# Weight sums through DRAM: the 16 GpSimd transfers written with the 128 rows outermost and the weight pairs inside

## The chip, the cores and the metric

One core of one Trainium2 chip runs the kernel. The metric is the device time of one execution in microseconds; it is the median of several runs. A profiled execution adds a page and a trace, whose times are counted in microseconds from the start of the span.

## What is computed

A decoder block over 1040 positions (16 meta tokens and 1024 tokens) of width 1024, all in float32:

```python
p = h @ w_in + b_in                     # columns: u_s5 | q | k | v | o | i | f | g_s5 | g_m
y_s5 = GLU(GELU(S5(u_s5)))              # grouped complex-diagonal state space model
y_m = (sigmoid(o) * HeadNorm(mLSTM(q, k, v, i, f))) @ m_w_out
mix = sigmoid(g_s5) * y_s5 + sigmoid(g_m) * y_m
h = LN(alpha * h + mix @ w_o)
h = LN(alpha * h + relu(h @ w_up + b_up)^2 @ w_down)
```

## The kernel before

Each float32 operand of the large products is split in two parts (`hi`, rounded, and `lo`, the rest), and a product is three matmuls, at L226, L227 and L228. TensorE (PE in the profile) runs these nearly without a gap. ScalarE (ACT) makes the `hi` parts, VectorE (DVE) the `lo` parts, so a weight tile `wraw` becomes `whi` (L212) and `wlo` (L213).

The two largest projections of the middle of the block, the mLSTM gate `g_m` and the output `m_w_out`, use seven products of half blocks in place of eight (class `Seven`). For that, sums and differences of weight blocks are needed. They are made without any compute engine: `w_sums` sends 16 DMA transfers from GpSimd's queue (POOL), from DRAM to DRAM into `ws_dr`, some of which copy and some of which add to what is there (`accum_op=OP.add`). There are eight for three pairs of tiles of `wf` (s = 0) and eight for four pairs of `wmo` (s = 1). One is issued with every second weight job from the fifth on: ahead of it POOL copies one element of the job's `whi` into `mark`, which makes POOL wait for that job. `Seven.load` fetches the results with SP's queue from about 698 us on.

All other bulk transfers are issued from SP's queue, one after the other in program order. Each takes one of eight completion semaphores in turn, and waits until the transfer that used it last has landed. So one slow transfer stops the queue eight transfers later.

Besides the jobs, the kernel runs side lanes, whose instructions a scheduler places between the matmuls. Three are spoken of here:
- The gates of the mLSTM (`gates`), near 100 to 150 us: short DVE and ACT steps on `gts`, with three small transposes on PE into `gps` (L421 is the last), then `gB` and `wiB` fetched by SP. Next to it `s5_pre` fetches the parameters `s_lam` of the state space model (L583), and DVE's first step with them is L557.
- `s5_gelu` for the fourth batch, near 566 to 598 us: `ys_dr` is stored, fetched back as `s5yc` in eight pieces (L871), put through GELU (`gelf`), and split into `gelh` (ACT) and `gell` (DVE, L878), on which the first job of the GLU waits.
- `ah_scale`, from about 528 us: eight row tiles `ahr` are fetched (L1377), multiplied and added (two DVE instructions at L1386), and stored to `ah_dr` (L1388). `up_early` follows it, on `wur`, `wpre` and `wu_dr`.

The GLU jobs (`z2s`, L940 to L945) use ACT and DVE to empty PE's accumulators; DVE's instructions stand in one fixed order, so an `ahr` that is late holds up a `z2s`.

Of the kernel before, what the change touches and what calls it, by code (L numbers as in the profile page):

```python
# [14 lines left out]
P = 128  # L15

D = 1024
KT = D // P
# [94 lines left out]
def decoder_block(  # L113
# [24 lines left out]
    def f32(ap):  # L138
        return ap.bitcast(F32)
# [816 lines left out]
    ws_dr = dram.tile([7, 4, P, 512], F32, name="ws_dr")  # L956

    def w_sums():
        todo = {}
        for s, (n0, p0, w, i0) in enumerate(((3, 0, wf, JGM + NM), (4, 3, wmo, 0))):  # L960
            def src(r, kh):
                return bass.AP(tensor=w.tensor, offset=w.offset + (i0 + r) * KT * P * P + 512 * kh,
                               ap=[[2 * KT * P * P, n0], [KT * P, P], [1, 512]])
            a11, a12, a21, a22 = src(0, 0), src(0, 1), src(1, 0), src(1, 1)
            d = [ws_dr[p0:p0 + n0, i] for i in range(4)]
            todo[s] = [(d[0], a21, 0), (d[2], a11, 0), (d[0], a22, 1), (d[2], a21, 1), (d[1], d[0], 0), (d[1], a11, 1),
                       (d[3], d[1], 0), (d[3], a12, 1)]
        mark = const.tile([1, 1], F32, name="mark")
        for s, i in ((0, 0), (0, 1), (0, 2), (0, 3), (0, 4), (1, 0), (0, 5), (1, 1), (0, 6), (1, 2), (0, 7), (1, 3),
                     (1, 4), (1, 5), (1, 6), (1, 7)):  # L970
            job = yield
            g_.tensor_copy(mark, f32(job.w[0][0][0:1, 0:1]))
            d, a, add = todo[s][i]
            tc.keep_in_program_order(g_.dma_start(d, a, accum_op=OP.add) if add else g_.dma_start(d, a))
# [442 lines left out]
    for w in ORDER.split():  # L1417
        n, i = w[0], int(w[1:])
# [22 lines left out]
    for w in LOAD0.split():  # L1441
        i = int(w[1])
# [21 lines left out]

    jobs = all_jobs
    ws = w_sums()
    next(ws)
    begin, first, run7 = gates_and_output()
# [609 lines left out]
```

## Time and profile before

| what | value |
|---|---|
| median of 3 runs | 1566.78 us (1564.85 to 1566.83) |
| the profiled execution, its own time | 1566.04 us |
| its span | 1564.2 us |
| PE busy | 1515.8 us, 97% |
| DVE busy, ACT busy, POOL busy | 1079.9, 642.7, 102.2 us |
| mean granted clock of PE | 0.984 |
| transfers of `w_sums` | 16, from 74.5 us to 602.1 us |

In the profile a line number is a line of the kernel. A row of the timeline gives the start, the duration, the engine, the line, the operation and its tiles; in brackets stands how long the engine sat idle before it and what ended that. SPq is SP's queue, and its rows are issues of transfers, not the moving of data. In a list of queues, q1 is what SP issued and q0 what POOL issued: packets, megabytes, and the share of the time of all 16 DMA engines.

### The profile page before, as it was taken

What the parts mean: (1) busy time and instruction counts of PE and PEld (TensorE: products, weight loads), DVE (VectorE), ACT (ScalarE), POOL (GpSimd) and SP (SyncE); (2) the same over time, 40 slices, a digit from 0 to 9 for tenths busy, and PEclk for the clock granted to TensorE, in tenths of its full rate; (3) what the DMA queues carried; (4) which work ended last, traced back from release to release, by engine and by line L of the source; (5) the groups of instructions that cost most, each with busy time, mean ns of one, the idle gap of its engine ahead of it and who ended that gap; (6) DMA issues with size and microseconds to landing.
All of it is one profiled execution on the core that took longest, in us unless ns stands there. A gap on an engine that the chain in (4) does not pass through costs nothing.

```text
span 1564.2 us, 20543 instructions
## 1 busy us (share of the span) xinstructions
PE 1515.8 (97%) x7593; PEld 1278.7 (82%) x7593; DVE 1079.9 (69%) x2083; ACT 642.7 (41%) x982; POOL 102.2 (7%) x195
## 2 busy tenths in 40 slices
PE   8999999998999998989999999999999999999997
PEld 8998988996878886768788887888888888888886
DVE  7667555659867845677789675666666679766786
ACT  6523353333355433325534324444444534433340
POOL 0000001124031200000000001000000000000000
PEclk9999999998999999989999999999999999999999
DMA  8412324414354556775353328644443798667642
GB/s 311 159 57 61 100 62 129 122 37 112 104 129 103 164 182 218 279 269 195 108 170 114 108 76 247 225 158 149 147 149 123 248 363 322 230 229 236 216 166 108
DMA packets 137509, 261.32 MB, mean 167 GB/s; under 512 B 30768, under 2 KB 52984, under 8 KB 137352
## 3 DMA queue, kind: packets, MB, share of 16 engines
q1 hardware_dynamic: 111344, 233.00, 43.7%
q0 software_dynamic: 26064, 27.01, 7.1%
q8 instruction: 60, 0.98, 0.3%
q14 instruction: 41, 0.34, 0.1%
HBM read 188.78 MB, written 84.55 MB: 175 GB/s over the span
## 4 chain that ended last, share of the span: by engine, by line
PE 31%; issue 23%; DMA 3%; DVE 2%; ACT 0%; SPq 0%; POOL 0%; POOLq 0%; DVEq 0%
PE mm L228 7%; PE mm L227 7%; PE mm L226 7%; PE sd L227 3%; PE sd L226 3%; PE sd L228 3%; DMA wpre<-wu_dr 1%; DMA rawb<-h_dr 1%; DMA wu_dr<-wpre 1%; DMA wur<-in_wup_dram 0%; DVE wlo L1043 0%; DVE wlo L213 0%; DMA woraw<-in_wo_dram 0%; POOL wpre L1621 0%; SPq L991 0%
## 5 line engine op out<-in xcount | busy, mean ns | idle before, releaser
L226 PE MATMUL mm<-hT_hi,whi 128*128 128x512 f32 (+3 forms) x604 | 231.0, 382 | 8.0 <-ACT whi L1042 5.4
L228 PE MATMUL mm<-hT_hi,wlo 128*128 128x512 f32 (+3 forms) x604 | 226.7, 380 | 5.7 <-DVE wlo L213 3.7
L227 PE MATMUL mm<-hT_lo,whi 128*128 128x512 f32 (+3 forms) x604 | 229.1, 379 | 0.0
L226 PEld LDWEIGHTS mm<-hT_hi,whi 128*128 128x128 f32 x604 | 115.7, 192 | 26.6 <-ACT whi L1042 6.2
L228 PEld LDWEIGHTS mm<-hT_hi,wlo 128*128 128x128 f32 x604 | 115.0, 191 | 25.5 <-DVE wlo L213 4.3
L227 PEld LDWEIGHTS mm<-hT_lo,whi 128*128 128x128 f32 x604 | 115.6, 191 | 17.6 <-issue 0.4
L227 PE MATMUL sd<-dwl,dah 128*128 128x512 f32 x240 | 94.5, 394 | 0.0
L228 PE MATMUL sd<-dwh,dal 128*128 128x512 f32 x240 | 94.4, 394 | 0.0
L226 PE MATMUL sd<-dwh,dah 128*128 128x512 f32 x240 | 94.2, 393 | 0.0
L1773 ACT ACTIVATE dah<-da 128x1024 fp32r<-128x1024 f32 x56 | 58.7, 1052 | 86.2 <-PE sd L227 38.9
L1777 ACT ACTIVATE dwh<-wdr 128x1024 fp32r<-128x1024 f32 x56 | 58.9, 1053 | 84.0 <-DMA wdr<-in_wdn_dram 27.5
L1774 DVE TENSOR_TENSOR dal<-da,dah 128x1024 fp32r<-128x1024 f32 x56 | 68.2, 1219 | 23.8 <-ACT dah L1773 23.3
L228 PE MATMUL mm<-dwh,dal 128*128 128x512 f32 (+1 forms) x224 | 84.5, 378 | 0.0
L226 PE MATMUL mm<-dwh,dah 128*128 128x512 f32 (+1 forms) x224 | 84.4, 377 | 0.0
L227 PE MATMUL mm<-dwl,dah 128*128 128x512 f32 (+1 forms) x224 | 84.3, 377 | 0.0
L1778 DVE TENSOR_TENSOR dwl<-wdr,dwh 128x1024 fp32r<-128x1024 f32 x56 | 68.2, 1219 | 13.1 <-ACT dwh L1777 12.4
L226 PE MATMUL mm<-whi,hT_hi 128*128 128x256 f32 (+1 forms) x256 | 75.2, 294 | 0.0
L228 PE MATMUL mm<-whi,hT_lo 128*128 128x256 f32 (+1 forms) x256 | 74.7, 292 | 0.0
L227 PE MATMUL mm<-wlo,hT_hi 128*128 128x256 f32 (+1 forms) x256 | 73.8, 288 | 0.0
L213 DVE TENSOR_TENSOR wlo<-wraw,whi 128x1024 fp32r<-128x1024 f32 (+1 forms) x46 | 56.1, 1222 | 19.1 <-ACT whi L212 18.6
L228 PE MATMUL mm<-th,wul 128*128 128x512 f32 x156 | 61.6, 395 | 0.0
L227 PE MATMUL mm<-tl,wuh 128*128 128x512 f32 x156 | 61.5, 394 | 0.0
(474 smaller groups left out, 3703.1 us busy)
## 6 DMA issues: line engine op xcount, KB each, us to landing
da<-act_dr SPq DMA_DIRECT2D x56, 512.0 KB, 5.4
wdr<-in_wdn_dram SPq DMA_DIRECT2D x56, 512.0 KB, 6.3
wur<-in_wup_dram SPq DMA_DIRECT2D x32, 512.0 KB, 4.3
act_dr<-upy SPq DMA_DIRECT2D x64, 256.0 KB, 2.5
wraw<-in_wf_dram SPq DMA_DIRECT2D x30, 512.0 KB, 6.9
wu_dr<-wpre SPq DMA_DIRECT2D x21, 512.0 KB, 4.7
wpre<-wu_dr POOLq DMA_DIRECT2D x21, 512.0 KB, 5.0
act_dr<-upx SPq DMA_DIRECT2D x32, 256.0 KB, 2.8
```

Of the source, the lines that this page charges most:

```text
L213: todo.append(lambda e=v_, r=r, hi=hi, lo=lo, n=n: e.tensor_tensor(lo[:, :n], r[:, :n], f32(hi[:, :n]), op=OP.subtract))
L226: t_.matmul(ps, ah, bh, start=(i == 0 and part[0]), stop=False, skip_group_check=skip)
L227: t_.matmul(ps, ah, bl, start=False, stop=False, skip_group_check=skip)
L228: t_.matmul(ps, al, bh, start=False, stop=(i == n - 1 and part[1]), skip_group_check=skip)
L1773: a_.activation(ah[:, :D], a[:, :D], AF.Copy)
L1774: v_.tensor_tensor(alo[:, :D], a[:, :D], f32(ah[:, :D]), op=OP.subtract)
L1777: a_.activation(wh, raw[i], AF.Copy)
L1778: v_.tensor_tensor(wl, raw[i], f32(wh), op=OP.subtract)
```

## The change

Only the access patterns of the 16 transfers change. Before, the outermost dimension of both sides is the pair (3 or 4 of them), then 128 rows, then 512 numbers. After, the 128 rows are outermost, the pairs come second, and the 512 numbers stay innermost. The same numbers go to the same places.

```diff
             def src(r, kh):
                 return bass.AP(tensor=w.tensor, offset=w.offset + (i0 + r) * KT * P * P + 512 * kh,
-                               ap=[[2 * KT * P * P, n0], [KT * P, P], [1, 512]])
+                               ap=[[KT * P, P], [2 * KT * P * P, n0], [1, 512]])
             a11, a12, a21, a22 = src(0, 0), src(0, 1), src(1, 0), src(1, 1)
-            d = [ws_dr[p0:p0 + n0, i] for i in range(4)]
+            d = [ws_dr[p0:p0 + n0, i].rearrange("n p c -> p n c") for i in range(4)]
```

The instructions of PE, DVE, ACT and SP stand in the same order as before, and so do POOL's. What differs is the shape of 16 of POOL's rows. The first piece is from POOL's order near 198 to 235 us of the profile; `v_...` are tiles of the mLSTM's values.

```order
 L972 COPY mark<-whi 1x1
-L974 DMA ws_dr<-in_wf_dram 3x128x512
+L974 DMA ws_dr<-in_wf_dram 128x3x512
 L336 MEMSET v_2267 128x1 x4
 L336 MEMSET v_3375 16x1
 L972 COPY mark<-whi 1x1
 L336 MEMSET v_2268 128x1 x4
-L974 DMA ws_dr<-ws_dr 3x4x16384
+L974 DMA ws_dr<-ws_dr 128x3x512
```

Nothing moved. A transfer within `ws_dr` used to have both inner dimensions in one run of 65536 numbers per pair, cut into four pieces of 16384; now it has 384 pieces of 512.

The second piece is the end of POOL's order, near 524 to 602 us.

```order
-L974 DMA ws_dr<-ws_dr 4x4x16384
+L974 DMA ws_dr<-ws_dr 128x4x512
 L972 COPY mark<-whi 1x1
-L974 DMA ws_dr<-in_wmo_dram 4x128x512
+L974 DMA ws_dr<-in_wmo_dram 128x4x512
 L972 COPY mark<-whi 1x1
-L974 DMA ws_dr<-ws_dr 4x4x16384
+L974 DMA ws_dr<-ws_dr 128x4x512
 L972 COPY mark<-whi 1x1
-L974 DMA ws_dr<-in_wmo_dram 4x128x512
+L974 DMA ws_dr<-in_wmo_dram 128x4x512
```

Nothing moved here either: two copies and two additions, each behind the `mark` of its job.

## The prediction

> **What bounds the kernel now.** I read the page first, then who waits for the 16 transfers, then PE's waits from 70 to 640 us, the time in which they run.
>
> ```profile
> PE 1515.8 (97%) x7593; PEld 1278.7 (82%) x7593; DVE 1079.9 (69%) x2083; ACT 642.7 (41%) x982; POOL 102.2 (7%) x195
> ```
>
> PE is the bound. The change touches no instruction of PE, DVE, ACT or SP, so it can gain only where PE stands still, or runs at a lower clock after standing still, because something came late through a DMA. What `ws_dr` holds is fetched from 698 us on, long after the last transfer, so nobody waits for the sums themselves. What counts is what the transfers do to others while they run.
>
> How long two of the copies and one of the additions take (issue time at the end of the first line, landing in the second):
>
> ```profile
> L974 POOL DMA_DIRECT2D ws_dr<-in_wf_dram x1: 1112/1112/1112, 104.2 to 104.2; - x1
> DMA to landing us min/median/max: 13.7/13.7/13.7
> ...
> L974 POOL DMA_DIRECT2D ws_dr<-in_wmo_dram x1: 1129/1129/1129, 267.7 to 267.7; - x1
> DMA to landing us min/median/max: 13.1/13.1/13.1
> ...
> L974 POOL DMA_DIRECT2D ws_dr<-in_wmo_dram x1: 1946/1946/1946, 490.3 to 490.3; - x1
> DMA to landing us min/median/max: 29.6/29.6/29.6
> ```
>
> Three pairs (768 KB) take as long as four (1024 KB): the time goes with the bytes of one pair, 256 KB, as if each pair had one DMA engine of its own. An addition takes twice as long. The queues say the same, here for 112.5 to 113, 113 to 113.5 and 115 to 115.5 us, beside a small fetch on SP's queue (q1):
>
> ```profile
> DMA packets 108, 0.06 MB, mean 115 GB/s; under 512 B 98, under 2 KB 98, under 8 KB 108
> q0 software_dynamic: 10, 0.04, 19.9%
> q1 hardware_dynamic: 98, 0.02, 18.7%
> ...
> DMA packets 9, 0.04 MB, mean 74 GB/s; under 512 B 0, under 2 KB 0, under 8 KB 9
> q0 software_dynamic: 9, 0.04, 18.0%
> ...
> q1 hardware_dynamic: 6, 0.00, 1.1%
> ```
>
> POOL's queue is busy 18 to 20% of 16 engines: 3 of 16 is 18.75%. And the fetch of SP sends 98 packets in the first half microsecond, then none, and its last few two microseconds later. I read that as follows: its share on the 13 free engines is done at 113, its share on the 3 others waits behind POOL's packets.
>
> [...]
>
> **What one engine's queue costs others, first place (A).** The small fetch is `s_lam`. SP, DVE, PE, and PE's clock there (the columns of the window: PE, PEld, DVE, ACT, POOL, clock, DMA share, GB/s):
>
> ```profile
> 111.48 0.33 SPq L583 DMA_DIRECT2D s_lam<-in_s5l_dram  x1
> ...
> 117.13 0.17 DVE L557 TENSOR_SCALAR s_t<-s_lam 128x16 f32<-128x16 f32 x1 [3.62 <-DMA s_lam<-in_s5l_dram]
> ...
> 124.75 0.27 PE L421 MATMUL gps<-ident,gts 36*128 36x36 f32 x1 [1.99 <-ACT gts L418]
> ...
> 120.00:130.00 10.00, 8.01 (x49) 6.99 (x48) 4.51 (x25) 5.72 (x9) 0.00 (x0) 0.83 0.20 58
> ...
> 147.75 0.70 PE L477 MATMUL pu<-v,kw 16*128 16x257 f32 x2 [1.47 <-ACT kw L460]
> ```
>
> DVE stands 3.62 us for `s_lam`. Its next steps, and ACT's after them, run without a gap up to the `gts` for which PE stands 1.99 us; then the clock is 0.83 over 10 us, 1.7 us lost. Together 3.7 us. The `kw` at 147.75 hangs on the same chain, through `gB`, fetched after `gts`.
>
> **Second place (B).** The fourth `s5_gelu` and `ah_scale`. A copy is issued at 570.1, now in 64 KB pieces, as the packets of an earlier one at 400 to 403 us show (0.33 MB in 5):
>
> ```profile
> q0 software_dynamic: 5, 0.33, 25.2%
> ...
> L974 POOL DMA_DIRECT2D ws_dr<-ws_dr x1: 588/588/588, 570.1 to 570.1; - x1
> DMA to landing us min/median/max: 13.5/13.5/13.5
> ```
>
> It lands at 583.6. What SP, DVE and PE do meanwhile (the landing is that of the store at 571.26):
>
> ```profile
> 571.26 0.32 SPq L1388 DMA_DIRECT2D ah_dr<-ahr  x1
> DMA to landing us min/median/max: 13.3/13.3/13.3
> ...
> SPq L871 <- DMA ah_dr<-ahr: 7.5, 1, 7.5
> ...
> 585.27 0.34 SPq L1377 DMA_DIRECT2D ahr<-ah_dr  x1
> 586.65 1.36 SPq L198 DMA_DIRECT2D wraw<-in_wglu_dram  x1
> 588.06 0.59 SPq L1377 DMA_DIRECT2D ahr<-ah_dr  x1
> ...
> 589.98 1.23 DVE L1386 TENSOR_TENSOR ahr<-ahr,gB 128x1024 f32<-128x1024 f32 x1 [14.80 <-DMA ahr<-ah_dr]
> 597.42 1.22 DVE L878 TENSOR_TENSOR gell<-gelf,gelh 128x1024 fp32r<-128x1024 f32 x1
> 602.86 1.23 DVE L1386 TENSOR_TENSOR ahr<-ahr,gB 128x1024 f32<-128x1024 f32 x1 [4.22 <-DMA ahr<-ah_dr]
> 605.37 0.69 DVE L944 TENSOR_TENSOR z2s<-mm,z2s 128x512 f32<-128x512 f32 x1
> ...
> 598.69 0.50 PE L227 MATMUL mm<-gell,whi 128*128 128x512 f32 x1 [3.15 <-DVE gell L878]
> 606.12 0.79 PE L226 MATMUL mm<-gelh,whi 128*128 128x512 f32 x1 [2.13 <-DVE z2s L944]
> ...
> 600.00:605.00 5.00, 3.99 (x12) 2.77 (x10) 2.11 (x2) 1.53 (x3) 2.08 (x2) 0.73 0.65 204
> 605.00:610.00 5.00, 3.88 (x10) 3.12 (x11) 4.06 (x6) 0.00 (x0) 0.00 (x0) 0.66 0.80 172
> ```
>
> The store lands at 584.5, a microsecond after the copy. SP's last piece of `s5yc` waits 7.5 us for it, and the `ahr` fetch behind it goes out at 585.27. DVE stands 14.80 us, does three pairs of `ahr` steps, then `gell`, for which PE stands 3.15 us; the last `ahr` holds up `z2s`, for which PE stands 2.13 us. With the lower clock (5 us at 0.73 and at 0.66, 3.0 us) 8.3 us are lost here.
>
> **The change, part by part.**
>
> POOL's issue. A transfer from `wf` or `wmo` has as many pieces of 512 as before: nothing. The four copies within `ws_dr` go from 12 or 16 pieces to 384 or 512; their issue may grow from 0.588 us to the 1.129 or 1.946 us of the others, at most 1.4 us each. POOL is 7% busy, and its next work waits for a later job: nothing, and if that cover were gone, 6 us of POOL's time.
>
> Landing of one transfer. No row has a DRAM-to-DRAM transfer on 16 engines. The nearest have 128 rows outermost, one on POOL's own queue with 512 KB, one on SP's with 1024 KB:
>
> ```profile
> wpre<-wu_dr POOLq DMA_DIRECT2D x21, 512.0 KB, 5.0
> wdr<-in_wdn_dram SPq DMA_DIRECT2D x8, 1024.0 KB, 9.7
> ```
>
> So a copy lands in 5 to 9.7 us in place of 13 to 14, an addition, at twice that, in 10 to 19 in place of 30. I take 6 and 11, nearer to the first, since that row is of the same queue.
>
> A. The copy issued at 104.2 is gone at 110, before `s_lam` goes out at 111.48. `s_lam` then lands at about 113.4, when its free engines had finished, and DVE's 3.62 us are gone. With 9.7 us the copy ends at 114 and DVE still gains about 2. PE cannot gain more than its 3.7 us, nor more than `kw` comes earlier, since it stands for that next: 3.6, between 2 and 3.6. The stretches behind it, up to 560 us, have DVE steps that themselves follow PE, so the gain is carried on.
>
> B. Without the 7.5 us wait the `ahr` fetch goes out at 577.8, lands after 589.98 - 585.27 = 4.7 us, and the first two pairs are over early. But the third `ahr`, at 588.06, stands behind a fetch of weights (586.65) that waits for PE's progress. It lands at 588.06 + 4.7 = 592.8, its pair takes (597.42 - 589.98) / 3 = 2.5 us, `gell` starts at 595.2, not 597.42: 2.2 us earlier. The last `ahr` is fetched after that pair is stored, so it and `z2s` come 2.2 us earlier too. PE gets to `z2s` sooner and stands there longer: what counts is the 2.2 at 606.12, not 3.15 + 2.13. Bounds: 0, if the third `ahr` lands no earlier, and the whole 8.3.
>
> Behind 610 us up to 698 PE waits little for anything but `begin`'s fetches, issued after the last transfer: nothing, though stores there may come out of the way earlier (0 to 2 in the range).
>
> Sum: 3.6 + 2.2 = 5.8 us from the profiled execution's own 1566.04, so 1560.2. The median lies 0.74 higher, so 1561.0.
>
> **The rivals.**
>
> Given back. The gain of A is used up where DVE itself is the limit, and B's next late step takes the place of the one removed. For it: PE's stall at `z2s` does grow. Against it: DVE ahead of those stretches waits for PE. The gain is then 0 to 2.2: 1565.6.
>
> All of B. If the `ahr` fetches come early enough that neither stall remains, 3.6 + 8.3 = 11.9: 1554.9. Against it: the third fetch's place behind the weights.
>
> Slower: all 16 engines together are slower than the three were. Now 768 KB in 13.7 us are 56 GB/s; below that the point is passed. At 48 GB/s, 16 us, `s_lam` comes 2.3 us later and the store in B too, on all engines: 2.3 + 2.3, so 1571.4. Against it: four pairs move a third more than three in the same time, so the sum has not been the limit. [...]
>
> No effect: the transfers stay on few engines: 1566.8. Against it: the two rows just quoted.
>
> **How the numbers follow.** The forecast 0.61, given back 0.16, all of B 0.13, slower 0.06, no effect 0.04. A measurement of this kernel can tell about 0.2%, 3.1 us. Faster by more: 0.56 of the 0.61 and 0.13, 0.69. Same: 0.05 + 0.16 + 0.04, 0.25, slower 0.06. The range takes in half of the case below and given back above: 1555 to 1566.3. The forecast's own, by its bounds (A 2 to 3.6, B 0 to 4): 1558.5 to 1564.
>
> **What would show it.** Copies of `ws_dr` landing in 5 to 8 us, additions in 9 to 14; q0 alone at more than 50% of 16 engines; no wait of DVE for `s_lam` above 1 us and none of PE at L421; the store near 571 landing in under 8 us, PE's stall at `gell` under 1.7 us, and one at `z2s` of more than 2. I am wrong if landings stay above 13 us, or if they shrink and PE's lost time at 125 and 600 us does not.

## The result, and the profile after

The changed kernel takes 1548.36 us, the median of 4 runs (1547.06 to 1548.64), against 1566.22 of the kernel before on the same chip: a ratio of 0.9885, 95% interval 0.9872 to 0.9898. It is faster, as forecast, but by 17.9 us where 5.8 were forecast; 1548.4 lies below the lower end of the range. The profiled execution has its own time of 1548.64 and a span of 1546.8.

The page's first part, and two answers on `ws_dr` from 60 to 640 us (how long its transfers took to land), first of the kernel before, then of the changed one; then POOL's queue alone, from 105 to 107 us in the changed kernel:

```profile
PE 1508.0 (97%) x7593; PEld 1275.0 (82%) x7593; DVE 1080.9 (70%) x2083; ACT 643.8 (42%) x982; POOL 97.7 (6%) x195
```

```profile
DMA to landing us min/median/max: 12.4/19.4/35.2
```

```profile
DMA to landing us min/median/max: 4.6/7.0/13.5
```

```profile
DMA packets 95, 0.39 MB, mean 195 GB/s; under 512 B 0, under 2 KB 0, under 8 KB 95
q0 software_dynamic: 95, 0.39, 69.6%
```

The transfers land in 4.6 to 13.5 us in place of 12.4 to 35.2 (the eight copies in 4.6 to 9.7, the additions in 6.8 to 13.5), and POOL's queue keeps 69.6% of 16 engines busy where it kept 18 to 20%. From 344 to 346 us POOL's queue alone shows 97.9% and 379 GB/s, where the form with three pairs outermost showed 18.0% and 74 GB/s from 113 to 113.5 us. So that part of the forecast holds.

PE's busy time fell by 7.8 us although it does the same work, and its mean granted clock rose from 0.984 to 0.988: the clock was low for less time.

Place A in the changed kernel: DVE, PE, and the window in which the clock was 0.83:

```profile
113.12 0.17 DVE L557 TENSOR_SCALAR s_t<-s_lam 128x16 f32<-128x16 f32 x1
143.17 0.70 PE L477 MATMUL pu<-v,kw 16*128 16x257 f32 x2 [0.72 <-ACT kw L460]
```

```profile
120.00:130.00 10.00, 10.00 (x79) 9.51 (x78) 3.71 (x17) 2.38 (x7) 0.00 (x0) 1.00 0.38 113
```

No bracket behind `s_lam`: DVE no longer waits for it. PE stands nowhere at L421, half as long at `kw`, and the clock is full. In two more executions of this kernel, taken later, the stall at `kw` is 1.09 and 0.73 us.

Place B, SP's queue and DVE, then all that PE waited for from 500 to 720 us (engine, line, who, us, times, longest):

```profile
558.22 0.32 SPq L1388 DMA_DIRECT2D ah_dr<-ahr  x1
566.98 0.85 SPq L1377 DMA_DIRECT2D ahr<-ah_dr  x1
569.54 0.93 SPq L198 DMA_DIRECT2D wraw<-in_wglu_dram  x1
570.52 0.70 SPq L1377 DMA_DIRECT2D ahr<-ah_dr  x1
...
581.14 1.23 DVE L878 TENSOR_TENSOR gell<-gelf,gelh 128x1024 fp32r<-128x1024 f32 x1 [1.36 <-ACT gelh L877]
591.65 0.69 DVE L944 TENSOR_TENSOR z2s<-mm,z2s 128x512 f32<-128x512 f32 x1 [4.04 <-PE mm L228]
```

```profile
PE mm L226 <- ACT whi L1042: 3.8, 1, 3.8
PE mm L228 <- DVE wlo L1043: 2.4, 1, 2.4
PE s5y L858 <- DVE s5w L846: 1.2, 1, 1.2
```

The stalls at `gell` and `z2s` are gone, and so are the five small ones from 640 to 670 us. DVE now waits for PE at `z2s`, not PE for DVE. The store that took 13.3 us near 571 us goes out at 558.22 and lands in 8.4, just over the 8 that the forecast gave it. The third `ahr` fetch goes out at 570.52, where it was 588.06; only 5.8 of these 17.5 us had been gained by 511 us.

To see where the time went, four marks cut the execution: the last `hT_hi` of the start (ACT, L1296), the `s5y` for which PE stands 1.17 us, the matmul that waits for `wlo` of `begin`, and PE's last matmul (at 1555.34 before, 1534.63 after). The first three, before, then after:

```profile
59.41 1.05 ACT L1296 ACTIVATE hT_hi<-hf 128x1024 fp32r<-128x1024 f32 x1
511.47 0.49 PE L858 MATMUL s5y<-s5w,s5RS 128*128 128x128 f32 x2 [1.17 <-DVE s5w L846]
698.63 0.79 PE L228 MATMUL mm<-hT_hi,wlo 128*128 128x512 f32 x1 [1.91 <-DVE wlo L1043]
```

```profile
59.10 1.05 ACT L1296 ACTIVATE hT_hi<-hf 128x1024 fp32r<-128x1024 f32 x1
505.64 0.49 PE L858 MATMUL s5y<-s5w,s5RS 128*128 128x128 f32 x2 [1.17 <-DVE s5w L846]
677.71 0.80 PE L228 MATMUL mm<-hT_hi,wlo 128*128 128x512 f32 x1 [2.36 <-DVE wlo L1043]
```

From the first mark to the second: 452.1 us before, 446.5 after, so 5.5 less. To the third: 187.2 and 172.1, 15.1 less. To the fourth: 856.7 and 856.9. From PE's last matmul to the end of the span (the tail): 8.9 (1564.2 - 1555.34) and 12.2 (1546.8 - 1534.63), 3.3 more.

The second stretch as one window, before, then after (the stretch, its length, then PE's busy time; the last three columns are the clock, the DMA share and GB/s):

```profile
511.47:698.63 187.16, 171.65 (x752) 137.48 (x752) 114.83 (x192) 64.44 (x91) 14.21 (x24) 0.96 0.68 228
```

```profile
505.64:677.71 172.07, 165.93 (x752) 135.41 (x752) 114.94 (x192) 64.91 (x91) 13.29 (x24) 0.99 0.74 246
```

PE stood 15.5 us before and 6.1 after, 9.4 less. Its 752 matmuls took 171.65 and 165.93 us, 5.7 less, at a clock of 0.96 and 0.99. So a good third of the 15.1 us is the clock: from 598 to 610 us, where PE stood for `gell` and `z2s`, it was 0.72 before; from 577 to 599 us it is 1.00 now.

What is longer in the tail is the DRAIN, an instruction that the queues of PE, ACT, DVE, POOL and SP have two or three times each at the end of the program (L2074); here is that of POOL's queue (count, shortest, median and longest in ns, first and last start); first before, then after, with SP's beside it:

```profile
L2074 POOLq DRAIN  x3: 46/98/3072, 1560.2 to 1563.9; - x3
```

```profile
L2074 POOLq DRAIN  x3: 46/97/6502, 1539.5 to 1546.5; - x3
L2074 SPq DRAIN  x3: 7/7/7, 1542.6 to 1546.2; - x3
```

SP's first DRAIN is done at 1542.6; POOL's began at 1539.5 and lasts 6.5 us in place of 3.07, and the end waits for it.

### The profile page after: what moved, and what is told of

It is laid out like the page before. It is cut to its first block, busy times and chain, and to the rows that moved or that the text cites. A ratio compares the mean times of both kernels' runs of the same rounds, so it can differ in the third digit from the quotient of the medians.

```text
span 1546.8 us, 20543 instructions
## 1 busy us (share of the span) xinstructions
PE 1508.0 (97%) x7593; PEld 1275.0 (82%) x7593; DVE 1080.9 (70%) x2083; ACT 643.8 (42%) x982; POOL 97.7 (6%) x195
## 4 chain that ended last, share of the span: by engine, by line
PE 30%; issue 24%; DMA 2%; DVE 1%; SPq 0%; POOL 0%; ACT 0%; POOLq 0%; DVEq 0%
PE mm L228 7%; PE mm L227 7%; PE mm L226 7%; PE sd L227 3%; PE sd L226 3%; PE sd L228 3%; DMA wpre<-wu_dr 1%; DMA rawb<-h_dr 1%; DVE wlo L1043 0%; SPq L991 0%; DMA woraw<-in_wo_dram 0%; POOL wpre L1621 0%; DVE hT_lo L1141 0%; DVE yp L1121 0%; DVE rawb L1002 0%
## 5 line engine op out<-in xcount | busy, mean ns | idle before, releaser
L213 DVE TENSOR_TENSOR wlo<-wraw,whi 128x1024 fp32r<-128x1024 f32 (+1 forms) x46 | 56.1, 1221 | 26.7 <-ACT whi L212 20.8
```

Of the source, the lines that this page charges most:

```text
L213: todo.append(lambda e=v_, r=r, hi=hi, lo=lo, n=n: e.tensor_tensor(lo[:, :n], r[:, :n], f32(hi[:, :n]), op=OP.subtract))
```

## The experiments

The first ones mix both forms. Each kernel is the one before with this line, and its own condition in place of `COND`:

```diff
-            d, a, add = todo[s][i]
+            d, a, add = [x.rearrange("n p c -> p n c") if type(x) is not int and COND else x for x in todo[s][i]]
```

(s, i) counts the transfers: (0, 1) is the copy near 104 us, (1, 4) to (1, 7) are those near 525, 538, 570 and 602. The table has the medians' ratio to the kernel before (95% interval), and of one profiled execution the four stretches cut above (the one to 511 begins at the first mark), and the longest DRAIN of POOL, in us. Each line of stretches is one execution; in the five of the changed kernel, two of them with one more DRAIN (at the end of this section), the second stretch is 171.1 to 172.1 us.

| kernel | 128 outermost | ratio | to 511 | to 698 | to PE's last | tail | DRAIN |
|---|---|---|---|---|---|---|---|
| before | none | 1 | 452.1 | 187.2 | 856.7 | 8.9 | 3.07 |
| after | all | 0.9885 (0.9872 to 0.9898) | 446.5 | 172.1 | 856.9 | 12.2 | 6.50 |
| e1_first | 104 | 0.9973 (0.9963 to 0.9984) | 447.8 | 186.8 | 856.5 | 8.9 | 2.83 |
| e2_last4 | 525, 538, 570, 602 | 0.9923 (0.9909 to 0.9938) | 452.2 | 171.0 | 857.2 | 12.1 | 6.42 |
| e3_rest | the other 11 | 0.9999 (0.9988 to 1.0010) | 451.5 | 185.7 | 857.1 | 9.4 | 3.72 |
| e4_570 | 570 | 0.9969 (0.9958 to 0.9980) | 450.6 | 181.3 | 857.9 | 8.8 | 3.19 |
| e5_adds | 538, 602 | 0.9923 (0.9898 to 0.9949) | 450.7 | 172.3 | 856.7 | 12.1 | 6.42 |
| e6_not538 | all but 538 | 0.9871 (0.9850 to 0.9893) | 448.7 | 172.9 | 856.5 | 8.9 | 3.07 |
| e7_not602 | all but 602 | 0.9912 (0.9891 to 0.9932) | 448.4 | 177.8 | 856.7 | 8.9 | 2.99 |
| e11_last | 602 | 0.9963 (0.9948 to 0.9977) | 452.0 | 179.5 | 857.1 | 10.9 | 5.28 |
| e10_three | 104, 570, 602 | 0.9901 (0.9883 to 0.9919) | 446.8 | 173.9 | 857.2 | 10.6 | 4.99 |
| again_after | all | 0.9888 (0.9870 to 0.9906) | 448.1 | 171.3 | 857.5 | 12.2 | 6.50 |
| again_not538 | all but 538 | 0.9877 (0.9860 to 0.9895) | 448.4 | 173.8 | 855.9 | 8.8 | 3.07 |
| third_after | all | 0.9893 (0.9876 to 0.9910) | 447.5 | 171.8 | 856.7 | 12.1 | 6.50 |

**Place A alone.** `COND`: `(s, i) == (0, 1)`.

> Only the copy issued near 104 us has the 128 rows outermost; the other 15 transfers are as before. Theory now (place A is worth 5.7 us: DVE's wait for `s_lam` and PE's stall at L421 go, the stall at `kw` L477 halves from 1.47 to about 0.7, and the clock near 120 to 160 us is not lowered): 1560.5 us, PE at any row from 340 us on 5 to 6 us earlier. Rival, the prediction's step (only the 3.6 us of the stall at L421 and its clock): 1562.6, `kw` stall at least 1.4. Second rival, that A's gain needs the transfers before it too: 1566, the `s_lam` wait stays over 3 us. POOL's last DRAIN (3.07 us before, 6.50 with all 16 changed): 3.3 if it grows with each transfer put on 16 engines, 3.07 if it grows with the number of pieces (here 384 in both forms).

Measured 1561.95 us; by the ratio 4.2 us faster (2.5 to 5.8), between what the two theories gave. The table says more: up to 511 us the six executions with an old copy near 104 us take 450.6 to 452.2, on average 451.5; those with the new one, 11 with the three kernels at the end of this section, 446.5 to 448.7, on average 447.8. Place A is worth 3.7 us. The 5.5 of the changed kernel's profile is the largest of the eleven.

The parts of the 3.7 us, from the same executions: PE's stall at L421 (1.76 to 2.13 us in the six, none in the eleven) gives 1.9; the one at `kw` (1.5 and on average 1.0) gives 0.5; the clock from 110 to 160 us fell for six pieces of 1.7 us in the six and for three in the eleven, which gives 1.2.

What spreads these numbers is the clock. In the kernel with the copy near 570 us alone, place A is as before, PE stands even longer at L421, yet the clock does not fall. First that kernel, then the one before, in which it did:

```profile
124.27 0.25 PE L421 MATMUL gps<-ident,gts 36*128 36x36 f32 x1 [2.13 <-ACT gts L418]
```

```profile
120.00:130.00 10.00, 7.87 (x61) 7.33 (x61) 4.06 (x24) 5.24 (x9) 0.00 (x0) 1.00 0.23 62
```

```profile
124.80:128.20 3.40, 3.40 (x17) 2.70 (x18) 0.81 (x7) 0.91 (x3) 0.00 (x0) 0.51 0.39 112
```

Before, the clock is at 0.51 for one piece of 3.4 us behind the stall of 1.99 us: 1.7 us. In the other kernel it is at 1.00 behind the stall of 2.13 us. What decides this is not shown: no run here moves a stall by itself. In these two executions a stall of 2 us cost 3.7 and 2.

**The rest.** `COND`: `(s, i) not in ((0, 1), (1, 4), (1, 5), (1, 6), (1, 7))`.

> The other 11 transfers have the 128 rows outermost; the copy near 104 us and the last four are as before. Theory now (all of the gain lies at these two places): no gain in front, stalls at L421, `gell` and `z2s` as before, and the end later by the DRAIN: 1567 to 1569. Rival (every shorter transfer gives its part of 20.7 us, 11 of 16): 1553. DRAIN: 5.4 us if by transfers on 16 engines, 4.8 if by pieces.

Measured 1565.62, the same as before (0.9988 to 1.0010). Eleven transfers in the form that lands in 4.6 to 10.3 us in the changed kernel, where these eleven took 12.4 to 29.6 before, change nothing beyond the 1.9 us that the interval leaves, with the others as they were. The DRAIN is 3.72 us, so neither count that was tried for it (by transfers, by pieces) holds.

**Place B alone.** `COND`: `(s, i) in ((1, 4), (1, 5), (1, 6), (1, 7))`.

> Only the last four transfers (issued near 525, 538, 570 and 602 us) have the 128 rows outermost. Theory now (the second place is worth 15 us, all of it from these four): no stall of PE at `gell` and `z2s` near 599 and 606 us, none above 0.5 us from 640 to 670, 15 us earlier at 698, and the end 14 us earlier for a longer DRAIN: 1552. Rival, the prediction's step (2.2 us, since the third `ahr` stands behind a fetch of weights that PE ties down): 1564. DRAIN of POOL: 3.9 us if by transfers on 16 engines, 4.8 if by pieces (two of the four copies within `ws_dr`).

Measured 1553.89, by the ratio 12.1 us faster. The second stretch is 16.1 us shorter, and 3.2 are given back in the tail. The prediction's 2.2 is refuted. The DRAIN is 6.42, where 3.9 or 4.8 was expected.

**The copy near 570 us.** `COND`: `(s, i) == (1, 6)`. This is the prediction's own mechanism for place B, by itself.

> Only the copy issued near 570 us (64 KB pieces before) has the 128 rows outermost. The prediction named this copy alone for place B. Its step: the store of `ah_scale` lands early, `gell` and `z2s` come 2.2 us earlier: 1564.0. Its rival, all of B: 8.3 us, 1557.9. Theory now: both stalls near 600 us go, since the fetch of weights in between is not tied to PE, but the additions near 538 and 602 us still hold up `ah_scale` ahead and the stores behind 605, so the stalls from 640 to 670 us stay: 6 to 8 us, 1559. If the additions are what matters alone: 1566, with DVE still over 10 us behind for `ahr`. DRAIN: 3.3 us if by transfers, 3.9 if by pieces.

Measured 1560.46, by the ratio 4.9 us faster (3.1 to 6.6). The second stretch is 5.9 us shorter. SP, DVE and PE in this kernel, then what SP's weights fetches waited for from 570 to 592 us in the kernel before:

```profile
577.09 0.43 SPq L1377 DMA_DIRECT2D ahr<-ah_dr  x1
578.56 1.41 SPq L198 DMA_DIRECT2D wraw<-in_wglu_dram  x1
580.02 0.51 SPq L1377 DMA_DIRECT2D ahr<-ah_dr  x1
...
588.90 1.22 DVE L878 TENSOR_TENSOR gell<-gelf,gelh 128x1024 fp32r<-128x1024 f32 x1
597.33 0.51 PE L226 MATMUL mm<-gelh,whi 128*128 128x512 f32 x1 [0.44 <-DVE z2s L944]
```

```profile
SPq L198 <- PE mm L228: 0.4, 1, 0.4
```

`gell` starts at 588.90 in place of 597.42, 8.5 us earlier; 2.1 of that had been gained by 511 us (0.6 ahead of the first mark, 1.5 behind it, about one piece of low clock, 1.7 us). PE does not stand at `gell` and only 0.44 at `z2s`; at the first `whi` of L212 it stands 2.92 us, where 1.7 in two stalls were lost before. With the second stretch as one window again, 3.8 of the 5.9 us are PE's standing and 2.1 its clock. The fetch of weights that the prediction held to be tied to PE goes out 8.1 us earlier with everything else: before, it had waited 0.4 us for PE.

**The two additions.** `COND`: `(s, i) in ((1, 5), (1, 7))`.

> Only the two additions issued near 538 and 602 us have the 128 rows outermost; the copy near 570 us stays in 64 KB pieces on four engines. With that copy alone changed PE was 8.0 us earlier at 698 us, 5.9 of it gained behind 511; with the last four 16.1, so about 10 us are left for the others. Theory now (the addition near 538 holds the `ahr` fetches ahead of the copy, the one near 602 the fetches of `up_early` behind it): DVE waits under 5 us for `ahr` up to 570, no PE stall from 640 to 670 above 0.5 us, yet the store near 571 still lands after 13 us: 6 to 10 us gained, 1556 to 1560. Rival, the prediction's step (additions at 538 and 602 cost PE nothing or up to 2): 1564 to 1566. POOL's DRAIN, which was 2.83, 3.72 and 3.19 us where the last one or more transfers kept their form and 6.42 where the last four changed: 6.4 if the last transfer's form sets it, about 4 to 5 if it is a matter of how many.

Measured 1553.24, below the 1556 to 1560 expected: nearly all of place B without touching the copy. DVE in this kernel, then when POOL issued the copy, in the kernel before and in this one:

```profile
579.94 1.23 DVE L1386 TENSOR_TENSOR ahr<-ahr,gB 128x1024 f32<-128x1024 f32 x1 [9.09 <-DMA ahr<-ah_dr]
587.44 1.22 DVE L878 TENSOR_TENSOR gell<-gelf,gelh 128x1024 fp32r<-128x1024 f32 x1
```

```profile
570.15 0.59 POOL L974 DMA_DIRECT2D ws_dr<-ws_dr  x1 [3.80 <-DMA ws_dr<-in_wmo_dram]
```

```profile
560.17 0.60 POOL L974 DMA_DIRECT2D ws_dr<-ws_dr  x1
```

DVE still waits 9.09 us there, for the copy is as slow as before (14.2 us to land), but 14.80 have become 9.09 and `gell` comes in time: PE does not stand. Two things are earlier ahead of it. DVE's waits for the two `ahr` ahead of the copy, 4.89 and 3.12 us before (near 562 and 568 us), are 0.80 and 0.89. And the copy itself goes out 10 us earlier: before, POOL stood 3.80 us in front of it until the addition near 538 us had landed, after 32.1 us; now that addition lands in 10.1.

**All but one.** `COND`: `(s, i) != (1, 5)`, and `(s, i) != (1, 7)`.

> All transfers but the addition near 538 us have the 128 rows outermost. What it costs alone is what the time stands above the 1548.4 of all 16. Theory now: it still holds the `ahr` fetches of 547 to 555 us for about 9 to 13 us each, DVE comes late, and PE stands at `gell` or `z2s` again, 2 to 5 us: 1550 to 1554. Rival (with the copy near 570 short, `ahr` catches up before PE needs `gell`): 1548, no PE stall at 585 to 600. DRAIN 6.4 if the last transfer sets it.

Measured 1545.97: the rival holds. The DRAIN is 3.07, not 6.4, though the last transfer has changed. With the copy short, the slow addition near 538 us costs PE nothing at `gell`; the second stretch is 172.9, 0.8 more than with all. `gell` starts at 587.45 us, as in the kernel with the two additions (587.44). So the addition near 538 and the copy near 570 can stand in for each other: PE was late at `gell` only where both were slow (3.15 us before, 1.2 with the other 11 changed).

> All transfers but the addition near 602 us (592 with the gain ahead of it) have the 128 rows outermost. Theory now: it lands about 32 us later and holds the stores and fetches of `ah_scale` and `up_early`, so stalls of 0.5 to 1 us at `whi` and `wlo` from 640 to 670 come back, 2.8 us with the clock's share more, and `begin` starts later: 1551 to 1554, less up to 3.4 for a shorter DRAIN. Rival, the prediction's step (nothing behind 610 matters, 0 to 2): 1548 or, with the shorter DRAIN, 1545 to 1546, which would be better than all 16. DRAIN 3.1 if the last transfer's form sets it, about 5.5 if it is a matter of how many.

Measured 1552.49, 6.5 us over e6_not538 and 4.1 over the changed kernel, in spite of a short DRAIN. PE's stalls near 628 to 642 us come back (1.8 us at `whi` of L212, 0.8 at `wlo` of L213), and the second stretch is 177.8, 5.7 more than with all.

**The addition near 602 us alone.** `COND`: `(s, i) == (1, 7)`.

> Only the addition near 602 us has the 128 rows outermost. Theory now: the stalls at `whi` and `wlo` from 640 to 670 us go and `begin` starts earlier, worth 5.7 us by itself, with the stalls at `gell` and `z2s` near 600 as before (3.15 and 2.13): 1560.5. Rival, the prediction's step (behind 610 us 0 to 2 us): 1564 to 1566. Second rival (`up_early` is late because `ah_scale` was late ahead of it, so the last addition counts only together with the copy near 570): stalls of 0.5 to 1 us from 640 to 670 stay, 1565.

Measured 1560.98, by the ratio 5.8 us faster (3.6 to 8.1). The second stretch is 7.7 us shorter. PE's waits from 580 to 700 us, and how long DVE and ACT stand in `up_early`:

```profile
PE mm L226 <- ACT whi L1042: 3.5, 1, 3.5
PE mm L227 <- DVE gell L878: 3.2, 1, 3.2
PE mm L228 <- DVE wlo L1043: 2.6, 1, 2.6
PE mm L226 <- DVE z2s L944: 2.1, 1, 2.1
```

```profile
617.80 0.69 DVE L1394 TENSOR_TENSOR wus<-wur 128x512 f32<-128x512 f32 x1 [2.86 <-DMA wur<-in_wup_dram]
624.37 0.63 ACT L1412 ACTIVATE wpre<-wus 128x512 fp32r<-128x512 f32 x1 [0.57 <-DMA wu_dr<-wpre]
```

The same in the kernel before, PE's waits from 560 to 700 us:

```profile
PE mm L226 <- ACT whi L1042: 5.4, 1, 5.4
PE mm L227 <- DVE gell L878: 3.1, 1, 3.1
PE mm L226 <- DVE z2s L944: 2.1, 1, 2.1
PE mm L228 <- DVE wlo L1043: 1.9, 1, 1.9
PE mm L226 <- ACT whi L212: 1.7, 2, 1.0
PE mm L228 <- DVE wlo L213: 1.1, 3, 0.5
```

```profile
622.96 0.69 DVE L1394 TENSOR_TENSOR wus<-wur 128x512 f32<-128x512 f32 x1 [5.70 <-DMA wur<-in_wup_dram]
633.45 0.63 ACT L1412 ACTIVATE wpre<-wus 128x512 fp32r<-128x512 f32 x1 [4.49 <-DMA wu_dr<-wpre]
```

`gell` and `z2s` are as late as before; the waits for L212 and L213 are gone, and `begin`'s first is shorter. Of the 7.7 us, 4.1 are PE's standing (15.5 to 11.4 us) and 3.6 its clock, with the stretch as one window again. Before, the addition was on its way for 35.2 us from 602 on, now for 11.7. With it on its way `wur` came later (DVE stood 5.70 us for it, now 2.86), the stores of `wpre` landed later, and ACT stood for them (4.49 us in the row above, 0.57 now); ACT's `whi` and DVE's `wlo` of the GLU jobs stand behind such rows and were late. That the addition costs this is shown by the run; the order of these steps is read from the waits. It is the transfer that the prediction gave nothing.

**Three of sixteen, and all but 538 once more.** `COND`: `(s, i) in ((0, 1), (1, 6), (1, 7))`; the other two kernels are known.

> Only three of the 16 transfers have the 128 rows outermost: the copies near 104 and 570 us and the addition near 602. Theory now: these three hold everything: PE 4 to 6 us earlier from the first, 14 more from the other two, DRAIN 3.1 since the addition near 538 is as before: 1546 to 1548. Rival (the other 13 are worth something together): 1551 or more.

> The changed kernel once more, for the comparison with the next one on the same chip. Theory now: 1548.4 us, DRAIN of POOL 6.5.

> All transfers but the addition near 538 us with the 128 rows outermost, once more. Theory now: PE is 0.8 us behind the changed kernel from 511 to 698 us, but POOL's DRAIN takes 3.07 us in place of 6.5 and the end waits for it, so 2 to 3 us faster than the changed kernel: 1546. Rival (the DRAIN is overlapped by something else that the end waits for, or differs from execution to execution): equal within 1 us, or 0.8 slower.

Measured 1550.93, 1549.24 and 1547.70. The first is slower than the 1546 to 1548 expected. The three transfers have all but about 2 us of the gain of PE's two first stretches: 5.2 and 13.3 us; the other thirteen make up these 2, as far as single executions can tell. Their DRAIN was 4.99, not 3.1, and how it comes out is not understood: it does not go by the number of changed transfers, nor by whether the last one is changed. The kernel with all but 538 changed has the lower median twice, by 2.4 and 1.5 us, but the intervals overlap.

**What the additions still cost.** In the changed kernel, additions made copies; the weight sums are missing.

```diff
-            tc.keep_in_program_order(g_.dma_start(d, a, accum_op=OP.add) if add else g_.dma_start(d, a))
+            tc.keep_in_program_order(g_.dma_start(d, a))
```

> The changed kernel with the eight additions made plain copies, so the weight sums are missing from what `Seven.load` fetches; each of these transfers should land in 5 to 6 us in place of 7 to 13.5. It asks what the new additions still cost. Theory now: nearly nothing, since PE does not stand from 511 to 673 us in the changed kernel: within 1 us of its 1549, apart from the DRAIN of POOL, which may be anything from 2.8 to 6.5 us. Rival (the additions still hold up `kw` near 143 us and `begin` near 674): PE 2 us or more earlier at 678, 1546.

Measured 1552.98, ratio 0.9921 (0.9906 to 0.9935): slower than with the additions. PE's stretches are 448.5, 171.4 and 856.9, as in the changed kernel, so the additions cost PE nothing any more. The 16 transfers land in 4.8 to 9.2 us, in the middle 5.8. The tail is 15.2 us, 3.0 more than in the changed kernel, for a DRAIN beyond the 2.8 to 6.5 us expected:

```profile
L2074 POOLq DRAIN  x3: 46/98/9523, 1541.8 to 1551.8; - x3
```

**The DRAIN.** POOL's queue has more transfers than the 16: it fetches `wpre` 21 times, 512 KB each, the last at 959.71 us in the changed kernel, so not all other bulk transfers are SP's. One more DRAIN of POOL in the changed kernel, first without a fixed place, then kept in program order behind the last fetch of `wpre` (the form shown):

```diff
-            fin["g"], fin["b"] = espot("g2B"), espot("b2B")
+            fin["g"], fin["b"] = espot("g2B"), espot("b2B"); tc.keep_in_program_order(g_.drain())
```

> The changed kernel with one more DRAIN in POOL's queue, near the start of the last stage, where POOL has had nothing to do since its last fetch of `wpre` and does nothing until the end. Theory: the DRAIN at the end clears up what POOL's own transfers left behind; the earlier one then lasts about 6 us beside PE's work, the last one under 0.2 us, and the end waits for SP's last store instead: the stretch from PE's last matmul to the end falls from 12.2 to about 8.5 us, 1545.5 us. Rival: the last DRAIN stays at 6.5 us whatever went before: 1549.

> The changed kernel a third time, as the neighbour of the kernel with the earlier DRAIN: 1549 us, the last DRAIN 6.5 us.

> The changed kernel with a DRAIN in POOL's queue right behind its last fetch of `wpre`, near 960 us (in the run before this one the added DRAIN had come to stand at 0.9 us, ahead of all transfers). Theory: the last DRAIN clears up what POOL's transfers left behind; the earlier one lasts 6 us or more (8 more for the last fetches to land) while POOL has nothing else to do, the last one under 1 us, and from PE's last matmul to the end it takes about 8.5 us in place of 12.2: 1545.3 us. Rival: the last DRAIN stays at 6.5 us whatever went before: 1549.

The first told nothing: the scheduler put the DRAIN at 0.9 us, ahead of all transfers, and the last one was 6.50 us as before (1549.06 beside 1548.57). The second is 1545.10 us (1544.74 to 1545.69), ratio 0.9868 (0.9851 to 0.9884). Its added DRAIN, and the last one:

```profile
L1993 POOLq DRAIN  x1: 10611/10611/10611, 960.2 to 960.2; - x1
```

```profile
L2074 POOLq DRAIN  x3: 34/98/1252, 1540.0 to 1543.7; - x3
```

The early one lasts 10.6 us while POOL has nothing to do (its last fetch lands 6.4 us after its issue at 960.19, so most of that may be the fetch). The last one takes 1.25, beside POOL's last compute instruction (L1885), which starts at 1540.00 too and takes 1.14. SP's first DRAIN starts at 1543.1, behind it now, and the tail is 8.8 us as in the kernel before: the 3.3 us are back. PE's stretches are 447.1, 171.1 and 856.6. All four of its runs lie below every run of the changed kernel (the lowest is 1547.06), so it is faster than that, though they ran on another chip and the interval of its ratio still touches that of the changed kernel.

## Why the prediction was right and wrong

- **The mechanism** was right: the new shape runs on 16 engines (97.9% at 344 to 346 us), and what was waiting behind the transfers is freed. No run shown ahead of the forecast had a DRAM-to-DRAM transfer on 16 engines; that the new shape would run on them was the author's estimate, with the times taken from the two rows with 128 rows outermost (5.0 and 9.7 us). The copies land in 4.6 to 9.7 us, in the middle 5.6 (6 forecast), the additions in 6.8 to 13.5 (11 forecast). The rival of a slow sum of all engines, below 56 GB/s, is refuted by 195 GB/s at 105 to 107 us.
- **Place A** was right in size: 3.6 forecast, 3.7 over 11 and 6 executions. That the sizes agree so well is in part luck. The sum had the stall at L421 and 1.7 us of clock, and nothing for `kw`; measured are 1.9, 1.2 and 0.5, and the clock fell behind L421 in two of the six executions only. The stretches behind it kept the gain, so "given back" fell too: the second stretch is 186.8 us with this copy alone and 187.2 before, and the third is 855.9 to 857.9 in every kernel.
- **Place B, the first step that failed**, was "the third `ahr`, at 588.06, stands behind a fetch of weights (586.65) that waits for PE's progress". The row of SP's waits has 0.4 us for it. The copy alone was worth 5.9 us, not 2.2: the stall at `gell` went, and the one at `z2s`, expected to grow beyond 2 us, fell to 0.44, as the rival "all of B" had it.
- **Nothing behind 610 us, the second step that failed**, was the larger miss: the addition near 602 us is worth 7.7 us by itself (0 to 2 forecast). The prediction took PE's waits there for little (1.7 and 1.1 us at L212 and L213) and `begin`'s for a matter of fetches issued after the last transfer. It did not ask what had held up the lane of `up_early` ahead of them.
- **The addition near 538 us** was not weighed at all. It made `ahr` late ahead of the copy, and it set the time of the copy: the prediction held that POOL's next work waits for a later job, but the copy at 570 us had waited 3.80 us for this addition to land. Together with the one near 602 it brings all of B, 14.9 us, though the copy stays slow; the difference to the 7.7 of that one alone is 7.2, not much more than the copy's 5.9, since either one made short frees `gell`.
- **POOL's issue**, feared to grow by up to 1.4 us for a copy within `ws_dr`, grew from 0.58 to 0.76 us, and that of the first copies from `wf` fell from 1.11 to 0.78. It played no part.
- **The end** was not foreseen: POOL's DRAIN takes 3.4 us more, and the end waits for it.

The sum as the runs have it: 3.7 at A, 15.1 to 15.9 in the second stretch (171.3 to 172.1 in three executions, all against one execution before, 187.2), less 3.3 in the tail: 15.5 to 16.3. The copy near 570 us and the addition near 602 us, each alone, make up 13.6 of the second term. The three comparisons of medians give 17.9, 16.9 and 16.5; the difference is of the size of one piece of low clock, 1.7 us, and not explained further.

## What to carry to other kernels

Where a queue's share of 16 engines stands near 3 or 4 sixteenths (here 18 to 20% with three pairs outermost and 25.2% with four), look at the outermost dimension of the transfer: here the rows outermost made copies land in 4.6 to 9.7 us in place of 12.4 to 13.7, with no other instruction changed. To price a slow transfer, list every transfer of the stretch with its landing, what its own queue waited for ahead of it, and what was issued in that time on other queues; the one nearest to the stall is not the only one that holds it, and of two that hold the same thing either may be mended. That a fetch "waits for PE" is read from the queue's own waits, never from its place in the order, and the end of the program has waits of its own (here POOL's DRAIN, 3.07 us before and 6.50 after).

## What the runs showed of the hardware that was not expected

POOL's DRAIN at the end of the program lasted 1.25 to 9.5 us in these kernels, though POOL had sent its last transfer 580 us before. It repeats for the same kernel (6.50 in three executions of the changed kernel, 3.07 in two with all but the addition near 538 changed) and changes with the shapes of transfers long done. With a DRAIN of one's own near 960 us the last one took 1.25 us in place of 6.50. What sets its length is open.

The store of 512 KB on SP's queue that went out while the copy near 570 us was on its way landed just behind it, in both forms of the copy: 0.6 to 1.0 us behind in the kernel before, the changed one and the three with the copy, the two additions, or all but the addition near 538 us changed. The store took 13.3 and 12.9 us beside an old copy and 6.6 to 8.4 beside a new one, where 3.0 is the median of the eight such stores in the changed kernel. So what the new form gave it is a copy that ended sooner (9.7 us in the changed kernel, 13.5 before).
